# Query and key products of an attention layer with the activations stationary, rotary on token rows, and transposes by TensorE

## The chip, the cores and the metric

The kernel runs on one core of a Trainium2 chip. The metric is the device time of one execution, in microseconds; the median of several runs is compared.

## The reference

A decoder trunk of two layers on one sequence of 256 tokens with 2048 features, all in float32. The first layer multiplies the input with one wide weight matrix whose columns feed a Mamba-2 mixer (z, x, B, C, dt) and 16 attention heads of 128 features (q, k, v, gate). With 256 tokens there is one attention block, so attention is plain causal attention:

```
z, xbc, dt, q, k, v, gate = split(x @ w_in)
q = apply_partial_rotary(q.reshape(b, s, 16, 128), pos)   # the first 32 of a head's 128 features
k = apply_partial_rotary(k.reshape(b, s, 16, 128), pos)   # x1, x2 = first 16, next 16
#   rot = [x1 * cos - x2 * sin, x1 * sin + x2 * cos]; the other 96 features pass
p = softmax(causal(q @ k.T * 128 ** -0.5))
y_b = (p @ v) * silu(gate)
x = layer_norm(alpha * x + concat(y_a, y_b) @ w_out)
```

The second layer is an S5 state-space mixer with a GLU (two gated products), and ends in the same kind of residual and layer norm. The change touches only q and k of the first layer.

## The kernel before, in words

**The weight stream.** All weights are laid out on the host as a list of units of 512 KB (128 partitions x 1024 float32), in the order of use. `split_to` (lines 218 to 243) loads a unit by SyncE's queue (`raw`), lets ScalarE (ACT, L239) round it to the matmul type fp32r (`wh`) and VectorE (DVE, L241) take the rest (`wl`), three units ahead of use with four buffers. Each product of activations x and weights w is the sum of three matmuls: high by high, high by low, low by high.

**Two forms of a product** (`product`, lines 310 to 326). Each has eight units of two 128-row pieces of the 2048 features, and fills two PSUM banks of 512 columns, which alternate with two others from product to product (`banks`).
- Kind "w" (`wmm`, L306): the weights are stationary, 128 columns of them at a time, and the 256 tokens move. A unit has 2 x 4 x 3 = 24 matmuls of 256 columns. The result has features on partitions and tokens along the row, which is what the scores need as an operand.
- Kind "x" (`xmm`, L285): the activations are stationary, 128 tokens at a time, and 512 weight columns move. A unit has 2 x 2 x 3 = 12 matmuls of 512 columns. The result has tokens on partitions, one bank for each half of the tokens.

A third form, `product_wide` (L339, L340), serves z, x, the gate and part of the second layer.

**The order of the work.** Around the products, small pieces of other work are queued as jobs. After each unit `pump` runs some: of the deque `jobs`, as many as spread what is there evenly over the units left of the product (lines 258 to 260), and of `back`, the slower background, by a count of units. DVE and ACT instructions of a job are placed behind the split of two units further on (`run`). The instruction order of each engine is then fixed ahead of time by a planner that simulates times; the engines themselves take their instructions in that order.

**The stage of the change** (lines 975 to 994). For each of four groups g of four heads: product q, product k, product v, then the gate by `product_wide`. q and k are of kind "w", v of kind "x". After q and after k, `rope_jobs` queues two jobs `rot`, one for each bank: ACT copies the 64 rows that pass (L907), DVE multiplies with cosine and sine tables (L908 to L910), and GpSimd (POOL) adds the two parts (L911). The host has permuted the columns of each head so that the rotated features are in rows 0 to 15 and 32 to 47. The attention jobs of a group (`score`, `turn`, `pv`) run in the next group's product q; its `turn` transposes the probabilities by TensorE (`transpose4`, L415) through one of four `aux` banks of PSUM.

In the background run, up to group 0, the head jobs of the Mamba mixer (they use the `b3` buffers, of which there are four), and from group 0's product v on the block jobs that build the tables of the second layer. Of those, `phasors` (L680 to L696) is a long chain of POOL instructions, which is placed behind the last rotary add queued so far (`turns`), and `pes` and `mts` (L749 to L780) use DVE, TensorE and `aux` banks.

In the second layer's GLU stage the jobs `gate, rest, rest, turn` (L1322) do for each product much what the change does here: arithmetic on token rows, a pause of two units, and four transposes in the next product's stream.

Of the kernel before, what the change touches and what calls it, by code (L numbers as in the profile page):

```python
# [11 lines left out]
AF = mybir.ActivationFunctionType  # L12
OP = mybir.AluOpType
# [3 lines left out]
P = 128  # L17
S = 256
# [28 lines left out]
def _fields(table, spec):  # L47
    at = 0
    for name, n in spec:
# [3 lines left out]


NCONST = _fields(CONST, [("ident", 128), ("causal", 256), ("tril", 128), ("shift", 384),
                         ("kmask", 16), ("sgn", 2), ("rope", 256), ("sel", 32)])
NPARAM = _fields(PARAM, [("convw", 96), ("convb", 24), ("normg", 16), ("ln0g", 16), ("ln0b", 16),
                         ("ssdd", 32), ("dtb", 1), ("alog", 1), ("s5d", 64)])

# [1 line left out]
def _constants():  # L61
    c = np.zeros((P, NCONST), np.float32)

    def put(name, a):
        lo, hi = CONST[name]
        c[: a.shape[0], lo:hi] = a.reshape(a.shape[0], -1)

    i = np.arange(P)
    put("ident", np.eye(P, dtype=np.float32))
    causal = np.zeros((P, 256), np.float32)  # L70
    causal[:, 128:] = np.where(i[None, :] <= i[:, None], 0.0, NEG)
    put("causal", causal)
    put("tril", (i[None, :] >= i[:, None]).astype(np.float32))
    sh = np.zeros((P, 3, P), np.float32)
    for t in range(1, 4):
        for r in range(P):
            if r % 4 + t < 4:
                sh[r + t, t - 1, r] = 1.0
    put("shift", sh)
    put("kmask", ((i[:, None] % 4 == 3) & ((i[:, None] // 4) % 16 == np.arange(16)[None, :])).astype(np.float32))  # L80
    sg = np.where(i < 64, -1.0, 1.0).astype(np.float32)
    put("sgn", np.stack([sg, -sg], 1))
    inv = np.float32(500000.0) ** (-(np.arange(16, dtype=np.float32) * np.float32(2.0) / np.float32(32)))
    ang = np.arange(S, dtype=np.float32)[:, None] * inv[None, :].astype(np.float32)
    cos, sin = np.cos(ang).astype(np.float32).T, np.sin(ang).astype(np.float32).T
    one, zero = np.ones_like(cos), np.zeros_like(cos)
    put("rope", np.concatenate([cos, one, cos, one, sin, zero, -sin, zero], 0))
    put("sel", np.tile(np.eye(32, dtype=np.float32), (2, 1)))
    return c

# [11 lines left out]
def _layout(inp):  # L102
    f = {k: np.asarray(v) for k, v in inp.items()}
    x = f["x"][0]
    a = {}
    a["consts"] = _constants()
    a["xt"] = np.ascontiguousarray(x.T.reshape(KT, P, S).transpose(1, 0, 2))
    a["xn"] = np.ascontiguousarray(x.reshape(2, P, 4, 512).transpose(2, 1, 0, 3))
    w = f["in0_w"][0]
    z, xs, b, c, dt = w[:, :2048], w[:, 2048:4096], w[:, 4096:4608], w[:, 4608:5120], w[:, 5120:5152]  # L110
    q, k, v, g = (w[:, 5152 + 2048 * i : 7200 + 2048 * i] for i in range(4))
    perm = np.concatenate([np.r_[0:16, 32:48, 16:32, 48:128] + 128 * h for h in range(16)])
    q, k = q[:, perm], k[:, perm]
    a["wdt"] = np.ascontiguousarray(dt.reshape(KT, P, 32).transpose(1, 0, 2))
    cols = [_half(xs), _half(z)]
    for h in range(4):
        hs = slice(512 * h, 512 * h + 512)
        cols += [_chunk(q[:, hs]), _chunk(k[:, hs]), _chunk(v[:, hs]), _half(g[:, hs])]
    b, c = _chunk(b), _chunk(c)
    first = np.stack([b[:PAIRED], c[:PAIRED]], 1).reshape(-1, P, UK * 512)  # L120
    a["wi0"] = np.concatenate([first, b[PAIRED:], c[PAIRED:]] + cols, 0)
    w = f["out0_w"][0].reshape(32, P, D)
    order = list(range(16, 28)) + list(range(16)) + list(range(28, 32))
    tail = list(range(16, 32)) + list(range(16))
    a["wo0"] = np.concatenate([_chunk(w[tail if c == 3 else order, :, 512 * c : 512 * c + 512].reshape(4096, 512)) for c in range(4)], 0)
    w = f["in1_w"][0]
    a["wi1"] = np.concatenate([_chunk(w[:, 0:512]), _half(w[:, 512:2048]), _chunk(w[:, 2048:])], 0)
    w = f["glu_w"][0]
    w = np.stack([w[:, :2048].reshape(D, 8, 256), w[:, 2048:].reshape(D, 8, 256)], 2)
    first = [0, 1, 2, 3, 4, 5, 8, 9, 10, 11, 12, 13, 6, 7, 14, 15]  # L130
    w = _chunk(w.reshape(D, 4096))
    a["wglu"] = np.concatenate([w[first], w[16:]], 0)
    a["wo1"] = _chunk(f["out1_w"][0])
    a["lnr"] = np.stack([f["ln_g"][0], f["ln_b"][0], f["ln_g"][1], f["ln_b"][1]])
    pr = np.zeros((P, NPARAM), np.float32)

    def put(name, m):
        lo, hi = PARAM[name]
        pr[: m.shape[0], lo:hi] = m.reshape(m.shape[0], -1)

    ft = list(range(16, 24)) + list(range(16))
    put("convw", f["conv_w"][0].T.reshape(24, P, 4)[ft].transpose(1, 0, 2))
    put("convb", f["conv_b"][0].reshape(24, P)[ft].T)
    put("normg", f["ssd_norm_g"][0].reshape(16, P).T)
    put("ln0g", f["ln_g"][0].reshape(16, P).T)
    put("ln0b", f["ln_b"][0].reshape(16, P).T)
    put("ssdd", np.broadcast_to(f["ssd_d"][0], (P, 32)))
    put("dtb", f["dt_bias"][0][:, None])
    put("alog", f["a_log"][0][:, None])

    def two(m):
        m = np.broadcast_to(m, (128, 64))[GORDER]
        dup = np.concatenate([m.T, m.T], 0)
        pair = m[SLOT].transpose(0, 2, 1).reshape(P, 64)
        return np.concatenate([dup, pair, pair], 1)

    a["s5p"] = np.stack([two(f["s5_lam_re"][0]), two(f["s5_lam_im"][0]), two(f["s5_log_dt"][0][:, None])], 1)
    d = f["s5_d"][0].reshape(128, 16)[GORDER].reshape(64, 2, 16, 1).copy()
    d[1::2] = d[1::2, ::-1].copy()
    put("s5d", np.broadcast_to(d, (64, 2, 16, 4)).reshape(64, P).T)  # L160
    a["params"] = pr
    br, bi = (f[n][0][GORDER].transpose(1, 0, 2) for n in ("s5_b_re", "s5_b_im"))
    cr, ci = (f[n][0][GORDER].transpose(2, 0, 1) for n in ("s5_c_re", "s5_c_im"))
    bc = np.stack([np.concatenate([br, bi], 0), np.concatenate([bi, br], 0), np.concatenate([cr, ci], 0)], 1)
    bc = bc.reshape(P, 3, 16, 8, 16).transpose(2, 0, 1, 3, 4)
    cs = np.stack([m.transpose(1, 0, 2)[SLOT] for m in (cr, ci)], 2)
    cs = cs.transpose(0, 3, 2, 1, 4).reshape(P, 2, 16, 4, 16).transpose(2, 0, 1, 3, 4).reshape(16, P, 1, 8, 16)
    a["s5bc"] = np.ascontiguousarray(np.concatenate([bc, cs], 2))
    return a


def trunk(tc, io, out):
    nc = tc.nc
    V, A, G, T = nc.vector, nc.scalar, nc.gpsimd, nc.tensor
# [6 lines left out]
    with ExitStack() as top:  # L181
# [10 lines left out]
        def C(name):  # L192
            lo, hi = CONST[name]
            return ct[:, lo:hi]
# [7 lines left out]
        def aux():  # L202
            return auxp.tile([P, 512], F32, tag="aux", name=nm("aux"))
# [41 lines left out]
        jobs = deque()  # L245
# [167 lines left out]
        def transpose4(dst, srcs):  # L413
            for i, s in enumerate(srcs):
                end = T.transpose(dst[:, i * P : i * P + P], s, ident)  # L415
            return end
# [24 lines left out]
        with ExitStack() as l0:  # L441
# [6 lines left out]
            def b3(shape):  # L448
                return wk.tile(shape, F32, tag="b3", bufs=4, name=nm("b3"))
# [44 lines left out]
            sel = cst.tile([P, 32], F32R, name="sel")  # L494
# [400 lines left out]
                    back.extend(skewed([head_jobs(k) for k in range(16)]))  # L895

            yb = {}
            cosb = C("rope")[0:64].unsqueeze(1).to_broadcast([64, 2, S])
            sinb = C("rope")[64:128].unsqueeze(1).to_broadcast([64, 2, S])

            def rope_jobs(ps, dst):
                def rot(i):
                    def go():
                        pv = ps[i].rearrange("p (f n) -> p f n", n=S)
                        q = dst[:, 2 * i : 2 * i + 2, :]
                        tm = b3([64, 2, S])
                        A.activation(q[64:128], pv[64:128], AF.Copy)  # L907
                        V.tensor_tensor(q[0:64], pv[0:64], cosb, op=OP.mult)  # L908
                        V.tensor_tensor(tm[0:32], pv[32:64], sinb[32:64], op=OP.mult)
                        V.tensor_tensor(tm[32:64], pv[0:32], sinb[0:32], op=OP.mult)  # L910
                        turns.append(G.tensor_tensor(q[0:64], q[0:64], tm, op=OP.add))  # L911
                    return go

                jobs.extend([rot(0), rot(1)])

            def attn_jobs(g, qT, kT, v, sg):
                for hp in range(2):
# [55 lines left out]
                    jobs.extend([score(0), score(1), turn(0), turn(1), pv])  # L973

            for g in range(4):
                ps = product("w", xhl)
                qT = a4([P, 4, S])
                rope_jobs(ps, qT)
                ps = product("w", xhl)
                kT = a4([P, 4, S])  # L980
                rope_jobs(ps, kT)
                ps = product("x", xhl)
# [409 lines left out]
```

## Time and profile before

| | |
|---|---|
| median of 3 runs | 1341.43 us (1340.94 to 1341.63) |
| the profiled execution | 1342.95 us |
| its span, from first to last instruction | 1341.1 us |
| TensorE busy (matmul; weight loads) | 99%; 86% |
| DVE, ACT, POOL busy | 75%, 51%, 28% |
| DMA | 211 GB/s in the mean |
| granted TensorE clock, mean | 0.998 |

A row of the grouped views names line, engine, operation, what is written from what, the shapes and the count; then the busy time in us and the mean duration in ns; then the idle time of the engine just before, and what ended it. A duration runs from an instruction's start to its end, and matmuls overlap, so the time that one takes from the engine is read from the start of one to the start of the next. A row of the chain of waits has the start, the length, the engine, the tile, the line and the count. A row of the windows has the stretch, its length, and each engine's busy time with the number of instructions.

### The profile page before, as it was taken

The numbers are of one execution on the slowest core, as the hardware profiler recorded it, in microseconds if no ns is written. First come the engines' busy times: TensorE is split into PE (matmuls) and PEld (weight loads), VectorE is DVE, ScalarE is ACT, GpSimd is POOL, SyncE is SP. The second block draws the span as 40 slices with busy tenths as digits, with TensorE's granted clock in tenths as the row PEclk, the third lists the DMA queues.
The fourth block names the chain that finished last, engine by engine and source line by source line (L and its number), as shares of the span: only waits on it lengthen the run. The fifth ranks groups of instructions, "written<-read, shape, count | busy, mean of one in ns | idle before, by whom it ended". The sixth has DMA issues, their size and how long they took to land.

```text
span 1341.1 us, 23054 instructions
## 1 busy us (share of the span) xinstructions
PE 1322.8 (99%) x8879; PEld 1151.2 (86%) x8879; DVE 1002.0 (75%) x1604; ACT 685.9 (51%) x914; POOL 371.7 (28%) x648
## 2 busy tenths in 40 slices
PE   9999999999999999999999999999999999999996
PEld 8988888998998998998888888898888888888885
DVE  5777977887788879789788765849899846555566
ACT  5566668864644553654564334344345644444441
POOL 0042000122027528627797600023343100000001
PEclk9999999999999999999999999999999999999999
DMA  8555555445546656756767778397989675565762
GB/s 315 179 170 181 187 173 173 156 144 174 172 149 231 217 175 212 243 186 203 235 197 248 240 245 296 131 322 240 313 283 320 203 221 188 188 190 188 253 218 77
DMA packets 80734, 282.88 MB, mean 211 GB/s; under 512 B 9840, under 2 KB 12528, under 8 KB 80112
## 3 DMA queue, kind: packets, MB, share of 16 engines
q1 hardware_dynamic: 68112, 239.33, 55.2%
q0 software_dynamic: 7328, 30.42, 6.7%
q10 hardware_dynamic: 5184, 11.67, 2.3%
q8 instruction: 69, 1.13, 0.4%
q14 instruction: 41, 0.34, 0.1%
HBM read 260.41 MB, written 20.97 MB: 210 GB/s over the span
## 4 chain that ended last, share of the span: by engine, by line
PE 85%; DVE 6%; DMA 3%; POOL 2%; issue 2%; ACT 1%; SPq 0%; POOLq 0%; DVEq 0%; ACTq 0%
PE main L285 40%; PE main L306 17%; PE main L339 14%; PE main L340 7%; DVE wl L241 2%; PE aux L415 1%; DMA raw<-in_wi 1%; DMA xr<-in_xn 1%; DMA raw<-in_wo 1%; PE aux L853 1%; PE enc L1188 1%; ACT wh L239 1%; PE dec L1233 1%; PE aux L764 1%; PE aux L962 1%
## 5 line engine op out<-in xcount | busy, mean ns | idle before, releaser
L241 DVE TENSOR_TENSOR wl<-raw,wh 128x1024 fp32r<-128x1024 f32 x431 | 537.1, 1249 | 273.2 <-ACT wh L239 268.8
L239 ACT ACTIVATE wh<-raw 128x1024 fp32r<-128x1024 f32 x431 | 455.7, 1059 | 537.9 <-PE main L285 268.3
L285 PE MATMUL main<-wh,A 128*128 128x512 f32 x1024 | 321.9, 392 | 0.0
L339 PE MATMUL main<-A,wh 128*128 128x512 f32 x768 | 272.0, 398 | 0.0
L285 PE MATMUL main<-wh,C 128*128 128x512 f32 x768 | 241.3, 392 | 0.0
L306 PE MATMUL main<-A,wh 128*128 128x256 f32 x1280 | 233.4, 286 | 1.6 <-ACT wh L239 1.3
L285 PEld LDWEIGHTS main<-wh,A 128*128 128x128 f32 x1024 | 191.9, 188 | 39.7 <-issue 0.3
L340 PE MATMUL main<-A,wl 128*128 128x256 f32 x768 | 215.6, 281 | 0.0
L306 PEld LDWEIGHTS main<-A,wh 128*128 128x128 f32 x1280 | 198.6, 192 | 3.5 <-ACT wh L239 1.5
L285 PE MATMUL main<-wl,A 128*128 128x512 f32 x512 | 200.2, 391 | 0.5 <-DVE wl L241 0.5
L306 PE MATMUL main<-A,wl 128*128 128x256 f32 x640 | 177.1, 284 | 0.0
L339 PEld LDWEIGHTS main<-A,wh 128*128 128x128 f32 x768 | 144.4, 188 | 33.7
L285 PEld LDWEIGHTS main<-wh,C 128*128 128x128 f32 x768 | 144.0, 188 | 30.5
L285 PE MATMUL main<-wl,C 128*128 128x512 f32 x384 | 149.8, 390 | 0.0
L340 PEld LDWEIGHTS main<-A,wl 128*128 128x128 f32 x768 | 145.0, 189 | 0.2
L306 PEld LDWEIGHTS main<-A,wl 128*128 128x128 f32 x640 | 120.7, 192 | 0.0
L691 POOL TENSOR_TENSOR c<-c 128x8 f32<-128x8 f32 (+2 forms) x192 | 106.8, 575 | 30.0 <-DMA wb<-c 22.4
L285 PEld LDWEIGHTS main<-wl,A 128*128 128x128 f32 x512 | 96.2, 188 | 20.2 <-DVE wl L241 0.8
L285 PEld LDWEIGHTS main<-wl,C 128*128 128x128 f32 x384 | 72.1, 188 | 14.7
L911 POOL TENSOR_TENSOR a<-a,b 64x512 f32<-64x512 f32 x16 | 30.2, 1891 | 166.8 <-ACT a L907 70.4
L339 PE MATMUL main<-C,wh 128*128 128x512 f32 x192 | 68.5, 401 | 0.0
L862 POOL TENSOR_TENSOR ssq<-ssq,c 128x256 f32<-128x256 f32 x16 | 15.3, 958 | 176.9 <-ACT c L860 176.2
(286 smaller groups left out, 1515.2 us busy)
## 6 DMA issues: line engine op xcount, KB each, us to landing
raw<-in_wi SPq DMA_DIRECT2D x271, 512.0 KB, 4.0
raw<-in_wo SPq DMA_DIRECT2D x96, 512.0 KB, 4.1
raw<-in_wglu SPq DMA_DIRECT2D x64, 512.0 KB, 3.5
wt<-wb POOLq DMA_DIRECT2D x16, 896.0 KB, 7.3
wb<-ob ACTq DMA_DIRECT2D x16, 512.0 KB, 5.7
bc<-in_s5bc SPq DMA_DIRECT2D x16, 256.0 KB, 4.2
wb<-c POOLq DMA_DIRECT2D x16, 256.0 KB, 3.3
wb<-om ACTq DMA_DIRECT2D x16, 128.0 KB, 4.9
```

The source lines that it names most:

```text
L239: high = A.activation(wh, raw, AF.Copy)
L241: splits[n] = (loaded[-1], high, V.tensor_tensor(wl, raw, wh.bitcast(F32), op=OP.subtract))
L285: T.matmul(ps[o], l[:, k, sl], r[:, j, :], start=start and i == 0, stop=stop and i == 2)
L306: T.matmul(pv[o // 2][:, o % 2, :], l[:, j, sl], r[:, k, :], start=first and i == 0 and o % 2 == 0, stop=end and i == 2 and o % 2 == 1, sk ...
L339: T.matmul(ps[o], wh[:, j, sl], xx[:, k, :, :].rearrange("p a n -> p (a n)"), start=first, stop=False, skip_group_check=True)
L340: T.matmul(ps[o][:, S : 2 * S], wl[:, j, sl], xh[:, k, :], start=False, stop=end, skip_group_check=True)
L415: end = T.transpose(dst[:, i * P : i * P + P], s, ident)
L691: G.tensor_tensor(p[:, :, :, 0:m], cs[:, :, :, 1 : m + 1], cs[:, i, :, n : n + 1].unsqueeze(1).to_broadcast([P, 2, 4, m]), op=OP.mult)
L764: T.matmul(pk[at : at + 64, 64 * n + a * 16 : 64 * n + a * 16 + 16], d["ev"][:, a, 64 * i : 64 * i + 64], cv[:, a, i, :], start=True, stop ...
L853: T.matmul(yo, xs[:, 0, xc], df[:, i, 0:256], start=True, stop=False)
L862: G.tensor_tensor(ssq, ssq, jk[:, f, :], op=OP.add)
L911: turns.append(G.tensor_tensor(q[0:64], q[0:64], tm, op=OP.add))
```

## The change

q and k become products of kind "x". Their results have tokens on partitions; the rotary then works on 32 columns of each of four heads in a bank, for one half of the tokens at a time, with a table of 64 columns a half (cos, cos, -sin, sin). The host no longer permutes the columns. The result `sb` stays in a `b3` buffer of 640 columns (512 for the rotated rows, 128 for the products with the sine); after two empty jobs, a job `turn` transposes its four heads by TensorE into an `aux` bank, and ACT copies that to `qT` or `kT`, which are as before.

```
-                         ("kmask", 16), ("sgn", 2), ("rope", 256), ("sel", 32)])
+                         ("kmask", 16), ("sgn", 2), ("rope", 128), ("sel", 32)])
...
-    one, zero = np.ones_like(cos), np.zeros_like(cos)
-    put("rope", np.concatenate([cos, one, cos, one, sin, zero, -sin, zero], 0))
+    put("rope", np.concatenate([cos, cos, -sin, sin], 0).T.reshape(2, P, 64).transpose(1, 0, 2))
...
-    perm = np.concatenate([np.r_[0:16, 32:48, 16:32, 48:128] + 128 * h for h in range(16)])
-    q, k = q[:, perm], k[:, perm]
...
-            cosb = C("rope")[0:64].unsqueeze(1).to_broadcast([64, 2, S])
-            sinb = C("rope")[64:128].unsqueeze(1).to_broadcast([64, 2, S])
-
             def rope_jobs(ps, dst):
-                def rot(i):
+                sb = {}
+
+                def rot(t):
                     def go():
-                        pv = ps[i].rearrange("p (f n) -> p f n", n=S)
-                        q = dst[:, 2 * i : 2 * i + 2, :]
-                        tm = b3([64, 2, S])
-                        A.activation(q[64:128], pv[64:128], AF.Copy)
-                        V.tensor_tensor(q[0:64], pv[0:64], cosb, op=OP.mult)
-                        V.tensor_tensor(tm[0:32], pv[32:64], sinb[32:64], op=OP.mult)
-                        V.tensor_tensor(tm[32:64], pv[0:32], sinb[0:32], op=OP.mult)
-                        turns.append(G.tensor_tensor(q[0:64], q[0:64], tm, op=OP.add))
+                        pv = ps[t].rearrange("p (h d) -> p h d", d=P)
+                        sb[t] = b3([P, 640])
+                        q = sb[t][:, 0:512].rearrange("p (h d) -> p h d", d=P)
+                        tm = sb[t][:, 512:640].rearrange("p (h d) -> p h d", d=32)
+
+                        def tab(lo, n):
+                            return C("rope")[:, 64 * t + lo : 64 * t + lo + n].unsqueeze(1).to_broadcast([P, 4, n])
+
+                        A.activation(q[:, :, 32:], pv[:, :, 32:], AF.Copy)
+                        V.tensor_tensor(q[:, :, 0:32], pv[:, :, 0:32], tab(0, 32), op=OP.mult)
+                        V.tensor_tensor(tm[:, :, 0:16], pv[:, :, 16:32], tab(32, 16), op=OP.mult)
+                        V.tensor_tensor(tm[:, :, 16:32], pv[:, :, 0:16], tab(48, 16), op=OP.mult)
+                        turns.append(G.tensor_tensor(q[:, :, 0:32], q[:, :, 0:32], tm, op=OP.add))
                     return go
 
-                jobs.extend([rot(0), rot(1)])
+                def turn(t):
+                    def go():
+                        px = aux()
+                        transpose4(px, [sb[t][:, h * P : h * P + P] for h in range(4)])
+                        A.activation(dst[:, :, t * P : t * P + P], px.rearrange("p (h n) -> p h n", n=P), AF.Copy)
+                    return go
+
+                rest = lambda: None
+                jobs.extend([rot(0), rot(1), rest, rest, turn(0), turn(1)])
...
             for g in range(4):
-                ps = product("w", xhl)
+                ps = product("x", xhl)
                 qT = a4([P, 4, S])
                 rope_jobs(ps, qT)
-                ps = product("w", xhl)
+                ps = product("x", xhl)
                 kT = a4([P, 4, S])
                 rope_jobs(ps, kT)
```

## The prediction, made before the changed kernel was run

> **What bounds the kernel now.** I read the chain of waits first, then the windows around the stage that is changed, then the single pieces of the chain. The page says that TensorE is never far from being the last to finish:
>
> ```profile
> span 1341.1 us, 23054 instructions
> ...
> PE 85%; DVE 6%; DMA 3%; POOL 2%; issue 2%; ACT 1%; SPq 0%; POOLq 0%; DVEq 0%; ACTq 0%
> ```
>
> 85% of the chain is TensorE. The changed stage runs from about 252 to 661 us: four groups g, each with the products q, k, v and the gate. In time order their windows are q0 and k0; q1 and k1; v1; q2 and k2; v2; q3 and k3; v3:
>
> ```profile
> core 0: us, PE busy (x) PEld busy (x) DVE busy (x) ACT busy (x) POOL busy (x), PEclk, DMA share, GB/s
> 252.50:307.50 55.00, 55.00 (x462) 52.51 (x461) 45.34 (x71) 37.77 (x60) 10.57 (x10) 1.00 0.48 152
> 354.20:406.90 52.70, 52.70 (x430) 52.08 (x429) 42.29 (x87) 28.60 (x44) 13.27 (x21) 1.00 0.50 162
> 406.90:432.60 25.70, 24.86 (x144) 20.51 (x144) 22.85 (x37) 11.02 (x15) 18.36 (x34) 1.00 0.62 197
> 455.20:510.50 55.30, 55.30 (x476) 54.69 (x475) 45.48 (x99) 30.18 (x49) 17.09 (x34) 1.00 0.53 175
> 510.50:536.10 25.60, 25.07 (x144) 20.39 (x143) 24.25 (x39) 10.70 (x12) 22.61 (x50) 1.00 0.65 221
> 558.40:614.10 55.70, 55.56 (x476) 54.69 (x475) 43.72 (x100) 30.53 (x49) 20.07 (x35) 1.00 0.59 185
> 614.10:635.90 21.80, 21.80 (x99) 18.08 (x98) 21.58 (x37) 9.70 (x10) 14.91 (x26) 1.00 0.66 211
> ```
>
> In the q and k windows TensorE is busy practically the whole time at full granted clock, DVE 78 to 82%, DMA about half: the matmul stream itself sets their length. The v windows, whose products already have the form that q and k are to get, are different: in v1, v2 and v3 DVE is busy 89, 95 and 99%, and in the first two TensorE has small holes. So the change is worth what it takes off TensorE's stream, and it must be asked separately what happens to DVE.
>
> **Part 1: the product form.** Eight products (q and k of four groups) of eight units each change from 24 matmuls of 256 moving columns a unit (L306) to 12 of 512 (L285): 1536 matmuls become 768, with the same columns streamed. The durations in the grouped rows are latencies that overlap, so I take spacing from long unbroken pieces of the chain, one of each form, next to each other:
>
> ```profile
> 266.33 5.75 PE main L306 x48
> ...
> 427.85 5.00 PE main L285 x22
> ...
> 594.21 20.16 PE main L306 x168
> 614.36 21.79 PE main L285 x96
> ```
>
> 20.16/168 is 120.0 ns for one of 256 columns; 21.79/96 is 227.0 ns for one of 512. Two narrow ones against one wide one: 240.0 - 227.0 = 13.0 ns, times 768 is 10.0 us. The other two pieces, of q0 and of v1, say 5.75/48 = 119.8 and 5.00/22 = 227.3: 12.3 ns a pair, 9.4 us. These come from busier surroundings, which q and k have too, and I take them: **-9.4 us**, with -10.0 as the other end.
>
> The Trainium skill ("TensorE: Matmul & The Clock Gate", section "Back-to-back issue gap") gives an isolated spacing of N/2.4 + 2.5 ns. An estimate from that page is 215.8 against 2 x 109.2 ns, 2.6 ns a pair and 2.0 us in all, less than the transposes cost, and the sum would turn to about +5 us. The two pieces above disagree with it: the part of the spacing that does not depend on the columns is 13 ns here (240.0 - 227.0).
>
> **Part 2: the transposes.** Each product gets two jobs `turn` of four 128x128 f32 transposes: 16 jobs, 64 transposes. The GLU stage does the same in a stream of the same L285 form, behind the same kind of pause (gate, rest, rest, turn):
>
> ```profile
> 1111.49 0.44 PE turn L415 x4
> 1111.93 7.98 PE main L285 x35
> ```
>
> There the four add 0.44 us to the chain and the stream goes on at once (7.98/35 = 228 ns). 16 x 0.44 = **+7.1 us**. Nothing hides this: it is TensorE's own time.
>
> The trace also gives the duration of one such transpose:
>
> ```profile
> L415 PE MATMUL turn<-consts,p x32: 270/272/273, 1111.3 to 1253.6; 128*128 128x128 f32 x32
> ```
>
> Taken as occupancy, 64 x 272 ns would be 17.4 us and the change a loss; the 0.44 us for four says that they are pipelined at 110 ns. The Trainium skill (the same page, "Part 4: PE-mode transpose") speaks against the change here: about 275 ns for one in a kernel, and transposes that do not count as activity for the clock gate. The duration agrees with the row, the cost does not follow from it, and where other matmuls surround them the clock stays at 1.00 (windows above, which hold the attention's own transposes).
>
> **Part 3: rotary on token rows.** Before, per half product: a copy on ACT, three multiplies on DVE, an add on POOL.
>
> ```profile
> L907 ACT ACTIVATE a<-main 64x512 f32<-64x512 f32 x16 | 9.5, 594 | 0.4
> L908 DVE TENSOR_TENSOR a<-main,consts 64x512 f32<-64x512 f32 x16 | 10.8, 674 | 0.0
> L909 DVE TENSOR_TENSOR b<-main,consts 32x512 f32<-32x512 f32 x16 | 10.9, 682 | 0.2
> L911 POOL TENSOR_TENSOR a<-a,b 64x512 f32<-64x512 f32 x16 | 30.2, 1891 | 166.8 <-ACT a L907 70.4 <-issue 60.6 <-DVE b L910 35.8
> L347 DVE TENSOR_TENSOR D<-D,main 128x256 f32<-128x256 f32 x32 | 13.2, 411 | 0.2 <-ACT D L346 0.2
> L691 POOL TENSOR_TENSOR c<-c 128x128 f32<-128x128 f32 x32 | 21.0, 675 | 1.3
> L797 ACT ACTIVATE C<-aux 128x512 f32<-128x512 f32 x8 | 4.6, 581 | 0.0
> ```
>
> Time goes with elements a partition. From 411 ns at 256 and 674 ns at 512 (both read PSUM) an estimate is 148 ns plus 1.03 ns an element, so 280 ns for the new 128x128 multiply and 214 ns for each 128x64: 0.71 us in place of 2.04 (L908 and twice L909, whose twin is L910), 1.33 us less DVE sixteen times, 21 us in all. POOL's add goes from 1.9 us to about 0.7 (L691). ACT's copy of 594 ns becomes one of 384 elements and so no longer, and each transposed tile needs a new copy like L797: 16 x 0.58 = 9.3 us more at most, with ACT busy 42 to 69% there. None of this lies on TensorE's path, so in the q and k windows it is worth nothing by itself.
>
> In the v windows it can be worth something, since k's rotary runs there on a DVE that is nearly full. Two holes show it:
>
> ```profile
> 425.69 0.39 PE L285 MATMUL main<-wl,A 128*128 128x512 f32 x1
> 426.91 0.94 PE L774 MATMUL aux<-kt,consts 128*128 128x128 f32 x6 [0.84 <-DVE kt L767]
> ...
> 527.36 0.48 PE L285 MATMUL main<-wh,A 128*128 128x512 f32 x1
> 528.37 0.49 PE L285 MATMUL main<-wl,A 128*128 128x512 f32 x1 [0.53 <-DVE wl L241]
> ```
>
> Start to start they are 1.22 and 1.01 us where 0.23 was due: some 1.0 and 0.8 us lost to DVE. 2.7 us less DVE in each v window can take both away: between 0 and -1.8 us. I take **-1.0**.
>
> The shorter units (12 x 0.227 = 2.73 us against 24 x 0.120 = 2.88) also ask a little more of the loads and of the two halves of the split of each weight unit:
>
> ```profile
> L241 DVE TENSOR_TENSOR wl<-raw,wh 128x1024 fp32r<-128x1024 f32 x431 | 537.1, 1249 | 273.2 <-ACT wh L239 268.8
> L239 ACT ACTIVATE wh<-raw 128x1024 fp32r<-128x1024 f32 x431 | 455.7, 1059 | 537.9 <-PE main L285 268.3
> ```
>
> 1.25 and 1.06 us fit into 2.73, and v3 ran at that pace, at 211 GB/s, with TensorE busy throughout though DVE was nearly full; the shorter unit adds some 4 points to DVE's share in the q and k windows, and the lighter rotary takes about as much back. No cost.
>
> **Part 4: the new wait.** Before, nothing on TensorE needed the rotary until the scores, a product or more later. Now `turn` waits on POOL's add, and behind a waiting transpose stand the next product's matmuls. `turn(0)` is fifth and `turn(1)` sixth in the next product's jobs, one a unit: 5 x 2.73 = 13.7 and 16.4 us behind its start. The slack can be read off the adds of before. The worst two products of groups 1 to 3 are k1 and k2, which ended at about 406.9 and 510.5 us:
>
> ```profile
> 415.65 1.28 POOL L911 TENSOR_TENSOR a<-a,b 64x512 f32<-64x512 f32 x1 [2.39 <-DVE b L910]
> 420.55 2.31 POOL L911 TENSOR_TENSOR a<-a,b 64x512 f32<-64x512 f32 x1 [3.62 <-DVE b L910]
> ...
> 509.87 0.12 POOL L683 MEMSET c<- 128x4 f32 x1
> ...
> 524.12 2.54 POOL L911 TENSOR_TENSOR a<-a,b 64x512 f32<-64x512 f32 x2
> ```
>
> One phasor chain of block jobs held POOL from 509.87 to 524.12, and both adds came behind it, the first done at about 525.4 (half of the merged 2.54 us), 14.9 us after the product's end, 1.2 us later than `turn(0)`'s place. k1's were done 10.0 and 16.0 us after its end, just in time; the other eight of the twelve came sooner. With shorter multiplies and adds they come sooner still. I take **+1.0** for all sixteen, between 0 and the rival's price below. `turn` also takes one of four `aux` banks until ACT has copied it, and a `b3` buffer for some four units instead of one; in group 0 the head jobs use the same four `b3` buffers, so these may run later, with no matmul of a product behind them: 0, at most +0.5.
>
> **The sum.** -9.4 + 7.1 - 1.0 + 1.0 + 0 = -2.3 us. The profiled execution took 1342.95 us, of which 1341.1 is the span; the median of the runs is 1341.43. Taken from the profiled execution that is 1340.65, from the median 1339.1. I say **1339.2**. A measurement of this kernel can tell about 0.2%, 2.7 us, from no change, so the likeliest result is a small gain at the edge of what can be seen.
>
> **Rivals.** *DVE relief.* The holes in the v windows vanish, no new ones come, and the pairs give their full 13 ns. For it: DVE at 89 to 99% there, and 21 us less of its work. Against: TensorE has no large hole in the q and k windows. It gives -10.0 + 7.1 - 1.8 = -4.7: 1336.7.
>
> *POOL becomes the bound of the turn.* The adds fall behind phasor chains, each about 14 us long, in the six products of groups 1 to 3, and TensorE stands at each turn. It decides from the point where an add ends later than 13.7 us behind the product. Before, one of twelve did, by 1.2 us. If each of six products pays that: +7.2, so -9.4 + 7.1 + 7.2 = +4.9 and 1346.3; a chain begun just ahead of the add could cost some 10 us in one place. For it: POOL is busy 68 to 88% in v1, v2 and v3, and the order on POOL is a planner's. Against: the same planner sets TensorE's order and can place the turn later.
>
> *Transposes cost their full duration*, 17.4 us, for want of cover around them: -9.4 + 17.4 = +8.0, 1349.4. The GLU stage speaks against it.
>
> *The change does not do what it says*: the new form's 13 ns a pair appear only in clean stretches and are lost between jobs. Then +7.1 remains with a few us back: about 1342 to 1345.
>
> **Chances.** The forecast's case 0.57, spread from -4.5 to +0.5: I give 0.20 of it to a gain beyond 2.7 us and 0.37 to no visible change. DVE relief 0.17, all faster. POOL 0.18, nearly all slower. Full duration 0.04, slower. Not as it says 0.04, half same and half slower. That makes faster 0.37, same 0.39, slower 0.24. The range runs from 1336.0, a little past the relief's end, to 1344.6, which takes in the lighter half of the POOL case; outside are the rest of it, the full duration, and a gain beyond 5.4 us: about 0.18.
>
> **What would show it.** Right: in the profile after, q and k windows of 96 wide matmuls at 227 to 228 ns; `turn` groups that add 0.44 us with no idle time behind POOL; DVE busy some 21 us less; a whole product with its two turns about 0.3 us shorter than before (1.17 less, 0.89 more). Wrong: idle time of TensorE ended by POOL or by ACT's copy at the turns; a spacing above 229 ns in the q and k windows; new holes at the scores or at the L774 matmuls.

## The result and the profile after

Over 22 runs each on the same chips the changed kernel took 1339.8 us in the median (1338.56 to 1345.0), the kernel before 1342.69 (1339.67 to 1345.35). The ratio is 0.9984 with a 95% interval from 0.9978 to 0.9990: 2.1 us faster, between 1.3 and 3.0; the two medians by themselves lie 2.9 us apart. The forecast was 2.2.

The page of the profile after, span and chain:

```profile
span 1339.7 us, 21680 instructions
...
PE 94%; POOL 2%; DVE 2%; DMA 1%; issue 1%; ACT 1%; SPq 0%; POOLq 0%; DVEq 0%; ACTq 0%
```

TensorE's share of the chain went from 85% to 94%, DVE's from 6% to 2%: where DVE had stood on the chain, the matmul stream now mostly runs through. The windows of the changed stage, in the order of those before (q0 and k0; q1 and k1; v1; q2 and k2; v2; q3 and k3; v3; the v windows start at the first matmul of v):

```profile
core 0: us, PE busy (x) PEld busy (x) DVE busy (x) ACT busy (x) POOL busy (x), PEclk, DMA share, GB/s
252.35:306.65 54.30, 54.30 (x277) 42.84 (x276) 40.88 (x71) 38.09 (x62) 11.16 (x10) 1.00 0.47 156
355.58:406.95 51.37, 51.37 (x247) 42.81 (x246) 37.53 (x89) 29.02 (x46) 15.33 (x31) 1.00 0.53 177
406.95:432.48 25.53, 25.53 (x151) 21.32 (x150) 17.74 (x37) 11.95 (x17) 16.45 (x43) 1.00 0.74 241
455.08:508.94 53.86, 53.86 (x292) 45.35 (x291) 41.34 (x100) 30.57 (x51) 20.84 (x51) 1.00 0.58 195
508.94:534.49 25.55, 25.55 (x152) 21.33 (x151) 17.73 (x38) 11.57 (x15) 22.08 (x47) 1.00 0.70 229
556.77:610.80 54.03, 54.03 (x292) 45.18 (x291) 40.78 (x101) 31.06 (x51) 11.09 (x31) 1.00 0.58 194
610.80:633.71 22.91, 22.91 (x106) 18.93 (x105) 17.96 (x35) 10.22 (x12) 16.08 (x35) 1.00 0.58 193
```

TensorE is busy in all of them without a hole, and DVE in v1 and v2 has gone from 89% and 95% to 69%. The q and k windows are shorter by 1.3 to 1.7 us in groups 1 to 3; v1 and v2 hardly changed, since they took in k's transposes and lost the holes; v3, which had none to lose, grew by 1.1 us.

Pieces of the chain in k1 and v1 (start, length, engine, tile, line, count):

```profile
389.78 8.18 PE main L282 x36
397.96 0.44 PE aux L412 x4
398.39 2.77 PE main L282 x12
401.16 0.44 PE aux L412 x4
401.60 16.37 PE main L282 x72
```

16.37/72 is 227.4 ns for a matmul of 512 columns, and each turn (four transposes, L412) puts 0.44 us into the stream and nothing else. The rotary's own instructions, grouped (L908 to L912), the new copy (L919), and the adds on POOL with their shortest, median and longest time:

```profile
L908 ACT ACTIVATE b<-main 128x384 f32<-128x384 f32 x16 | 7.5, 471 | 0.0
L909 DVE TENSOR_TENSOR b<-main,consts 128x128 f32<-128x128 f32 x16 | 4.5, 283 | 1.1 <-ACT b L908 1.1
L910 DVE TENSOR_TENSOR b<-main,consts 128x64 f32<-128x64 f32 x16 | 3.4, 212 | 0.0
L919 ACT ACTIVATE a<-aux 128x512 f32<-128x512 f32 x16 | 9.3, 581 | 0.0
L912 POOL TENSOR_TENSOR b<-b x16: 447/476/1700, 284.3 to 616.8; 128x128 f32<-128x128 f32 x16
```

The shortest slack between an add and its transposes was in v2 (timeline of POOL, then of TensorE):

```profile
515.95 0.49 POOL L912 TENSOR_TENSOR b<-b 128x128 f32<-128x128 f32 x1
...
522.64 0.60 PE L412 MATMUL aux<-consts,b 128*128 128x128 f32 x4
```

The add ends at 516.44 us and its turn starts at 522.64, 6.2 us later; the other fifteen had 8.1 to 14.6 us. No turn waited.

### The profile page after: what moved, and what is told of

Read it like the earlier page. It is cut to its first block, busy times and chain, and to the rows that moved or that the text cites. A ratio compares the mean times of both kernels' runs of the same rounds, so it can differ in the third digit from the quotient of the medians.

```text
span 1339.7 us, 21680 instructions
## 1 busy us (share of the span) xinstructions
PE 1324.2 (99%) x8175; PEld 1119.6 (84%) x8175; DVE 960.9 (72%) x1604; ACT 688.7 (51%) x930; POOL 336.6 (25%) x648
## 3 DMA queue, kind: packets, MB, share of 16 engines
q8 instruction: 64, 1.05, 0.3%
## 4 chain that ended last, share of the span: by engine, by line
PE 94%; POOL 2%; DVE 2%; DMA 1%; issue 1%; ACT 1%; SPq 0%; POOLq 0%; DVEq 0%; ACTq 0%
PE main L282 59%; PE main L336 14%; PE main L337 7%; PE main L303 5%; PE aux L412 2%; PE aux L850 1%; PE aux L761 1%; PE enc L1197 1%; PE dec L1242 1%; PE aux L939 1%; PE aux L971 1%; DVE wl L238 0%; DMA raw<-in_wi 0%; PE dec L1238 0%; POOL ew L527 0%
## 5 line engine op out<-in xcount | busy, mean ns | idle before, releaser
L282 PE MATMUL main<-wh,A 128*128 128x512 f32 x1536 | 489.9, 394 | 0.0
L282 PEld LDWEIGHTS main<-wh,A 128*128 128x128 f32 x1536 | 287.8, 188 | 59.1 <-issue 0.3
L282 PE MATMUL main<-wl,A 128*128 128x512 f32 x768 | 300.8, 392 | 0.0
L337 PE MATMUL main<-A,wl 128*128 128x256 f32 x768 | 215.4, 281 | 0.0
L336 PEld LDWEIGHTS main<-A,wh 128*128 128x128 f32 x768 | 144.2, 188 | 33.9
L282 PEld LDWEIGHTS main<-wl,A 128*128 128x128 f32 x768 | 144.3, 188 | 29.2 <-issue 0.5
L337 PEld LDWEIGHTS main<-A,wl 128*128 128x128 f32 x768 | 144.9, 189 | 0.2
L282 PEld LDWEIGHTS main<-wl,C 128*128 128x128 f32 x384 | 72.1, 188 | 14.6
L912 POOL TENSOR_TENSOR b<-b 128x128 f32<-128x128 f32 x16 | 10.2, 639 | 194.6 <-DVE b L911 152.1
L337 PE MATMUL main<-C,wl 128*128 128x256 f32 x192 | 53.8, 281 | 0.0
L690 POOL TENSOR_TENSOR c<-c,c 128x4 f32<-128x4 f32 (+2 forms) x96 | 48.0, 500 | 7.4
L303 PE MATMUL main<-A,wh 128*128 128x256 f32 x256 | 44.1, 288 | 1.5 <-ACT wh L236 1.5
L691 POOL TENSOR_TENSOR c<-c,c 128x4 f32<-128x4 f32 (+2 forms) x96 | 45.5, 474 | 0.0
```

The source lines that it names most:

```text
L282: T.matmul(ps[o], l[:, k, sl], r[:, j, :], start=start and i == 0, stop=stop and i == 2)
L303: T.matmul(pv[o // 2][:, o % 2, :], l[:, j, sl], r[:, k, :], start=first and i == 0 and o % 2 == 0, stop=end and i == 2 and o % 2 == 1, sk ...
L336: T.matmul(ps[o], wh[:, j, sl], xx[:, k, :, :].rearrange("p a n -> p (a n)"), start=first, stop=False, skip_group_check=True)
L337: T.matmul(ps[o][:, S : 2 * S], wl[:, j, sl], xh[:, k, :], start=False, stop=end, skip_group_check=True)
L690: G.tensor_tensor(cs[:, 0, :, n + 1 : n + 1 + m], p0[:, 0, :, 0:m], p1[:, 1, :, 0:m], op=OP.subtract)
L691: G.tensor_tensor(cs[:, 1, :, n + 1 : n + 1 + m], p0[:, 1, :, 0:m], p1[:, 0, :, 0:m], op=OP.add)
```

## The experiments

For each kernel I give the ratio to the kernel before, run beside it, and the length of each group's q, k and v window, from the first matmul of q to the first of the gate. These windows repeat to some hundredths of a microsecond between two profiles of one program, where the whole time of one program scatters by some microseconds (1338.56 to 1345.0 above), so they carry the reading:

| kernel | ratio, 95% interval | g0 | g1 | g2 | g3 | sum |
|---|---|---|---|---|---|---|
| before | 1 | 79.04 | 78.42 | 80.92 | 77.51 | 315.9 |
| changed | 0.9984 [0.9978, 0.9990] | 80.51 | 76.90 | 79.41 | 76.94 | 313.8 |
| changed, again | 0.9972 [0.9962, 0.9982] | 80.50 | 76.91 | 79.41 | 76.94 | 313.8 |
| no transposes | 0.9935 [0.9923, 0.9948] | 79.59 | 74.99 | 77.48 | 74.98 | 307.0 |
| transposes twice | 1.0039 [1.0027, 1.0052] | 82.26 | 78.57 | 81.05 | 78.69 | 320.6 |
| old form, light rotary | 0.9977 [0.9968, 0.9986] | 79.03 | 77.37 | 79.85 | 77.51 | 313.8 |
| no pause | 0.9964 [0.9951, 0.9978] | 78.13 | 76.90 | 79.44 | 76.86 | 311.3 |
| other buffers | 0.9981 [0.9971, 0.9990] | 80.54 | 76.88 | 79.39 | 76.93 | 313.7 |
| four empty jobs | 0.9982 [0.9972, 0.9991] | 80.60 | 76.89 | 79.35 | 76.95 | 313.8 |
| other buffers, no pause | 0.9961 [0.9946, 0.9975] | 78.22 | 76.88 | 79.41 | 76.87 | 311.4 |
| q and k wide | 0.9959 [0.9947, 0.9972] | 77.6 | 77.7 | 78.5 | 76.3 | 310.1 |
| q wide, k in rows | 1.0084 [1.0062, 1.0107] | 77.8 | 79.2 | 92.9 | 76.7 | 326.7 |

**What form and transposes cost.** The first kernel leaves out the transposes, the second does each twice ("..." stands for what is left out of a line):

```
-                        px = aux()
-                        transpose4(px, [sb[t][:, h * P : h * P + P] for h in range(4)])
-                        A.activation(dst[...], px.rearrange(...), AF.Copy)
+                        A.activation(dst[...], sb[t][:, 0:512].rearrange(...), AF.Copy)
```

> The changed kernel without its 64 transposes: turn copies the rotated rows to qT and kT as they lie, so the scores are of other numbers; all else is the same. Theory (the wide form gives 9.4 us, the transposes cost 7.1 us of TensorE's own time): 7 us faster than the changed kernel, 9 us faster than before, ratio to before 0.993. Rival (the wide form gives only some 2 us, since only 2.6 ns of each matmul do not depend on the columns, and the transposes are hidden): no different from the changed kernel, ratio 0.998. Rival (each transpose takes its full 272 ns, so that the form must have given near 19 us): 17 us faster than the changed kernel, ratio 0.985.

```
                         transpose4(px, [sb[t][:, h * P : h * P + P] for h in range(4)])
+                        transpose4(px, [sb[t][:, h * P : h * P + P] for h in range(4)])
```

> The changed kernel with each group of four transposes done twice into the same bank. Theory: 7.1 us slower than the changed kernel, 5 us slower than before, ratio to before 1.004. Hidden transposes: no different from the changed kernel, 0.998. Full duration: 17 us slower than the changed kernel, 1.011.

Medians 1333.77 and 1347.56 us. From none to once is 6.7 us in the windows, from once to twice 6.8: near the straight line of the theory (7.1), and neither hidden nor 17. Group 0 is apart: the transposes cost 1.91 to 1.96 us in each of the groups 1 to 3, but group 0 got only 0.92 us shorter without them, because other work there took longer (below), so the 6.7 understates them. Group 1 without, with and with twice the transposes, each from its own profile:

```profile
355.19:430.18 74.99, 74.99 (x380) 62.56 (x379) 55.89 (x125) 41.08 (x63) 30.42 (x67) 1.00 0.60 201
355.58:432.48 76.90, 76.90 (x396) 64.13 (x395) 55.27 (x125) 40.97 (x63) 31.79 (x74) 1.00 0.60 199
357.95:436.52 78.57, 78.57 (x412) 65.88 (x411) 55.37 (x125) 41.06 (x63) 31.19 (x70) 1.00 0.58 194
```

16 matmuls more each time (396, 412), and 1.91 and 1.67 us.

**What DVE's relief is worth by itself.** The kernel before, with most of the rotary left out:

```
-            sinb = C("rope")[64:128].unsqueeze(1).to_broadcast([64, 2, S])
+            sinb = C("rope")[0:64].unsqueeze(1).to_broadcast([64, 2, S])
...
-                        V.tensor_tensor(tm[0:32], pv[32:64], sinb[32:64], op=OP.mult)
-                        V.tensor_tensor(tm[32:64], pv[0:32], sinb[0:32], op=OP.mult)
-                        turns.append(G.tensor_tensor(q[0:64], q[0:64], tm, op=OP.add))
+                        V.tensor_tensor(tm[:, 0, 0:64], pv[0:64, 0, 0:64], sinb[:, 0, 0:64], op=OP.mult)
+                        turns.append(G.tensor_tensor(q[0:64, :, 0:64], q[0:64, :, 0:64], tm[...], op=OP.add))
```

> The kernel before (stationary weights in q and k) with most of the rotary left out: of the three multiplies of each half one stays whole and one of 64x64 stands for the other two, and the add on POOL covers 64x128 only. That takes some 18 us off DVE and some 20 us off POOL and changes nothing on TensorE, so q and k are of other numbers. Theory: of the changed kernel's gain only the holes that DVE left in v1 and v2 come from this, 1 to 2 us: ratio to before 0.999. Rival (the whole gain of the change is DVE's and POOL's relief, and form and transposes cancel): as the changed kernel or more, 0.998 to 0.996. Rival (those holes are filled from elsewhere): 1.000.

The ratio is 0.9977: as much as the whole change, and more than my theory had. The windows tell why. Groups 0 and 3, which had no hole in v, did not move; groups 1 and 2 got 1.05 and 1.07 us shorter, all of it in v1 and v2. Another 0.6 us goes around the first layer's layer norm (850 to 857 us), more than 200 us after the last rotary; but the wide kernel below, which keeps the three multiplies of each rotary, is 0.5 us shorter there too, so it isn't shown that DVE's relief makes this part. The chain through v1 of this kernel has no DVE left in it:

```profile
407.79 10.91 PE main L285 x48
418.70 0.87 PE aux L415 x8
419.57 1.04 PE aux L764 x32
420.62 5.68 PE main L285 x24
426.29 0.67 PE aux L774 x6
426.96 5.26 PE main L285 x23
```

But it does not follow that form and transposes cancel. This kernel has the relief and the old form; the one without transposes has the relief and the new form. Against the first the second is shorter: groups 1, 2 and 3 by 2.38, 2.37 and 2.53 us. On TensorE these two kernels differ there in the form alone, so that is what it gives: 2.43 us a group or 12.6 ns a pair, 9.7 us for four. Only group 0 breaks the rule: 79.03 became 79.59, where 76.6 was due.

**What group 0 lost.** Without the pause the changed kernel is 1337.42 us:

```
-                jobs.extend([rot(0), rot(1), rest, rest, turn(0), turn(1)])
+                jobs.extend([rot(0), rot(1), turn(0), turn(1)])
```

> The changed kernel without the two empty jobs between rot and turn, so that the turns come two units (5.5 us) sooner. In the trace of the changed kernel the adds on POOL end 6 to 14.6 us before their first transpose. Theory (the wait on POOL costs nothing, and the pause is longer than needed): the same as the changed kernel within 1 us, ratio to before 0.998. Rival (the slack is what keeps POOL off the path; a planner that sets the order in advance is a little wrong each time): the 16 turns wait 0.3 to 1 us each, 5 to 15 us slower than the changed kernel, 1.002 to 1.010.

The theory was right that nothing waits, but it expected no gain, and group 0 fell from 80.5 to 78.1. The turns stood closer behind their adds, the closest again in v2, where the add ended at 514.88 us and its turn started at 515.64, 0.8 us later. The chain shows what differs. Both pieces show one step of the head jobs late in group 0 (L850 and L851 are its matmuls, of 64 output rows, 16 of them a step), first in the changed kernel, then in the one without the pause:

```profile
318.12 0.59 PE aux L850 x4
318.71 0.22 PE aux L851 x4
318.93 0.43 PE main L282
319.36 0.58 PE aux L850 x2
319.94 0.22 PE aux L851 x2
320.15 0.89 PE main L282 x3
321.05 0.57 PE aux L850 x2
321.62 0.22 PE aux L851 x2
```

```profile
320.21 0.59 PE aux L850 x4
320.81 0.22 PE aux L851 x4
321.02 0.47 PE aux L850 x4
321.50 0.22 PE aux L851 x4
```

I call a visit a stretch of these matmuls that nothing else interrupts. Four of them alone take 0.80 us, as long as eight together (0.81), and the wide matmul behind them takes 0.2 us more than its 0.227. So 16 in one visit are 1.5 us, and cut into three 2.8. Over group 0 the visits number 7 before, 9 in the changed kernel, 10 in the one without transposes, 6 without the pause; what the window holds beside product matmuls (0.2273 and 0.1199 us each) and turns (0.45 each) goes with them: 11.2, 13.2, 14.1 and 10.9 us. The two visits more than before are the 2.1 us. The price of a visit is not constant: from six to seven the step is 0.3 us, from seven to nine 1.0 each, from nine to ten 0.9, and in the rows above 1.3 us for two. The Trainium skill ("TensorEngine Tiling (Array Packing)", section "Key Properties") says that a change of the tiling mode drains TensorE; the rows agree with a price for each visit, though no run here takes the mode apart from the wait for the first result.

Why the planner cuts more often I tried with the buffers and with a longer pause:

```
-                        sb[t] = b3([P, 640])
+                        sb[t] = a4([P, 640])
```

> The changed kernel with the rotated rows in a buffer of the a4 kind in place of b3, with the pause of two empty jobs kept. In the changed kernel the rows hold b3 buffers over the pause, the head jobs of group 0 wait for them, and their matmuls come in more and smaller pieces; group 0's q, k, v window took 80.5 us against 78.1 without the pause. Theory (it is the buffer): the head jobs come in as few pieces as without the pause, the window falls to about 78 us, 2.4 us faster than the changed kernel, ratio to before 0.9965. Rival (the earlier turn itself is what helped): as the changed kernel, 0.998.

```
-                jobs.extend([rot(0), rot(1), rest, rest, turn(0), turn(1)])
+                jobs.extend([rot(0), rot(1), rest, rest, rest, rest, turn(0), turn(1)])
```

> The changed kernel with four empty jobs between rot and turn in place of two, so that the rows hold their b3 buffers some 5.5 us longer. Theory of the buffer: group 0 gets worse once more, its window 81 to 84 us, 1 to 3 us slower than the changed kernel, ratio to before 0.999 to 1.001; groups 1 to 3 unchanged. Rival (group 0's loss is by chance of the order): within 0.7 us of the changed kernel either way.

My theory of the `b3` buffers fell: with others the window is 80.54 us with nine visits, with a longer pause 80.60 and nine. Both together, other buffers and no pause, came next:

> The changed kernel with the rotated rows in a4 buffers and without the pause. The a4 buffers alone left group 0 as it was (80.5 us, nine pieces of head-job matmuls), taking the pause away brought it to 78.1 us and six pieces. If the earlier turn is what helps, whatever the buffers: 78 us, six or seven pieces, ratio to before 0.9965. If it was the chance of one order: 79 to 80.5 us, eight to ten pieces, 0.997 to 0.998.

78.22 us, six visits, ratio 0.9961. So the early turn helps whatever the buffers, and the length of a pause does not matter once there is one. What in the planner's order makes the cuts stays open.

**Two ways on.** The third form for both q and k (shown for q; k is changed alike, the host lays out both as it does the gate, and the rotary reads its rows from SBUF):

```
-                ps = product("w", xhl)
                 qT = a4([P, 4, S])
-                rope_jobs(ps, qT)
+                product_wide(xhl, lambda qT=qT: qT, lambda h: None)
+                rope_jobs(qT)
```

> The kernel before with q and k by the third form, product_wide (weights stationary, high and low of the activations side by side as 512 columns, then 256 more), which leaves features on partitions and needs no transposes; the rotary then works on SBUF, and ACT and DVE add the two halves. In the trace of before the gate in this form takes 22.3 to 22.7 us a product, against 24 x 8 x 0.120 = 23.0 for the old form and 21.8 + 0.9 = 22.7 with transposes for the changed one. Theory (TensorE's stream sets the time): 0.5 us less a product, 4 us less than before, ratio 0.997, a little better than the changed kernel. Rival (DVE, nearly full in the v products, becomes the bound, since it gets 1.6 us more a product and no lighter rotary): holes in k and v products, 0 to 10 us slower than before.

1336.83 us, with the ones without the pause the best here of those that leave nothing out; their intervals overlap. By the table the windows are 5.8 us shorter, but the gate ahead of group 3 took 23.3 us in place of 22.3, so 4.8 us are left. Theory and rival both hold in part: v1 still has a hole of 1.6 us behind DVE, in a window where DVE is 89% busy:

```profile
404.51:431.00 26.49, 24.94 (x144) 20.44 (x143) 23.66 (x40) 10.14 (x14) 21.27 (x40) 1.00 0.61 201
```

The last kernel joined it, for q, with token rows without a pause for k (their rotary table comes as an input of its own):

> The two better forms joined: q by product_wide with the rotary on its feature rows (as in the run with both so), k as in the changed kernel but without the pause. In the run with q and k both wide the one large hole left (1.7 us in v1) stood behind DVE's rotary of k; the lighter rotary on token rows takes it away. Theory: q gives 0.5 us a product, k 1.2 less 0.9, the holes of before go: about 5 to 6 us less than before, ratio 0.9955, as good as either or a little better. Rival (the gain of each came from the chance of the planner's order in group 0): 0.997 to 0.998.

It took 1354.45 us, ratio 1.0084 [1.0062, 1.0107], which neither side expected. Timelines of TensorE and of POOL in v2, with some of POOL's rows, and two windows:

```profile
516.42 0.39 PE L289 MATMUL main<-wl,A 128*128 128x512 f32 x1
528.16 1.12 PE L419 MATMUL aux<-consts,b 128*128 128x128 f32 x4 [11.36 <-POOL b L938]
```

```profile
516.73 0.12 POOL L690 MEMSET c<- 128x4 f32 x1
...
527.66 0.45 POOL L938 TENSOR_TENSOR b<-b 128x128 f32<-128x128 f32 x1
```

```profile
516.00:529.00 13.00, 1.64 (x9) 1.18 (x7) 4.61 (x12) 1.06 (x1) 10.79 (x32) 0.63 0.32 108
529.00:543.00 14.00, 14.00 (x88) 11.51 (x87) 6.53 (x11) 5.24 (x7) 10.06 (x27) 0.86 0.37 126
```

The multiplies of k2 were done at 511.1 and 516.0 us, but a whole phasor chain stood in front of their adds on POOL (516.73 to 527.66). The turn waited 11.4 us with the product behind it, and the granted clock fell to 0.63 and 0.86 in the mean of the two windows. In v1 a turn waited 2.7 us behind its add (at 415.2 us), with no loss of clock. Group 2 is 13.5 us longer than in the kernel with other buffers and no pause, group 1 2.4 us. This is the prediction's rival of the POOL queue, at the price it gave for a chain begun just ahead of an add, some 10 us. It did not come in the changed kernel, where the same chain began behind the adds, in v2 half a microsecond after the second of them had started (517.25 against 516.76 us). The Trainium skill ("TensorE: Matmul & The Clock Gate", Part 1) says that TensorE falls back to half its clock after an idle window of some 3.4 us; the rows agree, with a fall after 11.4 us and none after 2.7.

## Why the prediction was right

- *Form, -9.4 us*: measured 12.6 ns a pair, 9.7 us, by the two kernels whose TensorE work differs in the form alone in groups 1 to 3. The 12.3 ns of the trace's own pieces decided rightly. By the estimate from the Trainium skill ("TensorE: Matmul & The Clock Gate", section "Back-to-back issue gap"), 2.6 ns a pair, the change would have been a loss.
- *Transposes, +7.1 us*: 6.7 and 6.8 us by the sums of the windows. Where the head jobs don't disturb the reading, it is 1.91 to 1.96 us a group in groups 1 to 3, and four turns of 0.45 us in group 0: 7.6 us. The occupancy (0.44 us for four), not the duration (272 ns each), is the price, as the GLU stage had shown.
- *DVE*: 283, 212 and 213 ns for the multiplies, estimated at 280 and 214. But the holes were mis-sized: -1.0 was taken and -1.8 was the bound, and the relief gave -2.1 in v1 and v2, a little more than the two holes that I had read. A further -0.6 at the layer norm, where I had not looked, is not in the forecast at all, and its cause is open. DVE's busy time on the page fell by 41 us (1002.0 to 960.9), of which the rotary's own rows give 21 (32.6 to 11.3), as forecast; most of the rest is other instructions that each got a little shorter, and no run here takes their cause apart.
- *The new wait, +1.0*: nothing. Every add was 6 us or more ahead. The shorter multiplies made that, as argued; I should have taken 0, with the rival as the tail: the last run showed that it is real, at 2.7 and 11.4 us.
- *Head jobs of group 0, 0 to +0.5*: this is the step that failed. I said that no matmul of a product stands behind them, and overlooked that they run on TensorE themselves: cut into nine visits instead of seven they cost 2.1 us of its time.

The sum of the measured terms is -9.7 + 7.6 - 2.1 - 0.6 + 0 + 2.1 = -2.7 us. The windows and the layer norm show the same (-2.1 and -0.6); in groups 1 to 3 this is so by construction, and group 0 tests the term of the head jobs. Two undisturbed profiles, before and the changed kernel again, have spans of 1341.1 and 1337.9 us, 3.2 apart; of this 0.5 stands ahead of the first q, whose start also differs by 0.35 us between the two profiles of the changed kernel. The forecast's sum, -2.3, lies near -2.7 by luck in part: against it the form gave 0.3 more, the transposes cost 0.5 more, the holes and the layer norm gave 1.7 more, the wait cost 1.0 less, and the head jobs cost 2.1 more. That the gain is as large as the relief's alone is such a chance too: form and transposes leave -2.1, and the head jobs of group 0 take 2.1 back.

## What to carry to other kernels

Where TensorE is never idle, count its stream: matmuls by start-to-start spacing, and every visit of side work by what it adds to the chain, since the same instructions can cost much more when a schedule cuts them into pieces (here sixteen of them 2.8 us in place of 1.5). A step that used to be off the path and now feeds TensorE through another engine's queue is only as safe as its slack in that queue; read the slack after each change, since a small change of order can use it up at once.

## What the runs showed of the hardware

The first profile of the changed kernel has a short loss of clock at the layer norm, which the second one does not have (the columns are those of the windows above; the granted clock is 0.69):

```profile
862.00:866.00 4.00, 2.73 (x14) 2.73 (x14) 4.00 (x7) 0.35 (x1) 0.00 (x0) 0.69 0.60 219
```

TensorE had stood for 1.6 us there, as it does in the kernel before and in the second profile of the changed kernel, where the clock stays at 1.00. In this profile matmuls of 256 columns then came every 213 ns, in place of 120, for some 3.4 us, and the stage took 1.5 us longer. The profiles of the kernel with four empty jobs and of the last kernel show the same loss at the same place; the other nine do not. The Trainium skill ("TensorE: Matmul & The Clock Gate", Part 1) names an idle window of about 3.4 us for a fall to half clock; the time at half clock agrees, but the hole ahead of it was half as long as that, and in the other profile the same hole had no such effect. Just ahead of the hole stand twelve transposes, 1.7 us long, with two matmuls behind them; whether the clock counts them as work is not settled by any run here. The two profiles of one program, spans 1339.7 and 1337.9 us, differ mostly by this, so one such event is nearly as large as the effect that was measured.
